# Up projection: one 512-column matmul for the high weights, the two halves of a bank added afterwards

## The chip, the cores and the metric

The kernel runs on one core of a Trainium2 chip. The metric is the device time of one execution in microseconds (us). Engines are named as in the profile: PE (matrix products), PEld (its weight loads), DVE (elementwise work on vectors), ACT (activations and casts), POOL, and SP, which issues the weight loads from memory.

## What is computed

One decoder layer on 256 tokens of width 2048. The part that matters here is the feed-forward block: the normalised rows are multiplied by `w_up` (2048 x 11264), convolved over three tokens, gated, and multiplied by `w_down`.

```python
def conv_ffn(h, w_up, ffn_conv_w, w_down):
    u = causal_dwconv3(h @ w_up, ffn_conv_w)
    g, val = jnp.split(u, 2, axis=-1)
    return (jax.nn.silu(g) * val) @ w_down
```

Before it come the modulation (`c_act @ w_mod`), the input projection, a gated convolution and linear attention, and the output projection; they are the same in both kernels.

## The kernel before

Every float32 operand is split into a high part (rounded to fp32r) and a low part (what is left), and a product is the sum of three: high weights by high activations, high weights by low activations, low weights by high activations.

The work is a list of units, run in order by `drive` (L69). A unit is one block of weights. It has `prep` (SP loads the block into one of six raw buffers, ACT casts it to the high part `wh`, one of three buffers), `low` (DVE subtracts to get the low part `wl`, one of three buffers, L145), `mm` (the products on PE) and `fin` (what follows the group's last unit, spread over the units behind it). While unit i is at its products, the list has already issued the load and cast of unit i + 2 and the low part of unit i + 1. Each engine works through its own list in order.

The up projection has 22 groups of four output tiles (4 x 128 columns of `w_up`); a group below 11 is a gate, group g + 11 its value. `up_units` (L827) makes units of four k-tiles. The activations `h2` hold two k-tiles in one buffer, each as 256 high and then 256 low columns. The products go to four PSUM banks `pss`, 256 float32 columns of each, for one group. A unit has 4 k-tiles x 4 outputs x 3 = 48 products of 256 columns (L854).

A first pass runs ten groups over k-tiles 0 to 7 (mode `part`, two units a group): their sums are copied by ACT (L795) into a buffer `part`. In the second pass these ten come back for k-tiles 8 to 15 (mode `rest`, two units): DVE adds the bank to the kept sum (L801). The other twelve groups run all 16 k-tiles in one go (mode `all`, four units) and are read straight from PSUM. The second pass goes by ORD: gate 0 and value 11 (both `rest`), gate 5 and value 16 (both `all`), 1 and 12 (`rest`), 6 and 17 (`all`), and so on. After each group come `first`, `second` and `third` of `ffn_stages` (L780), in that many following units: ACT scales the sum by the middle tap (L806), DVE adds the two other taps (`taps`, eight operations through L136, four at a time for `all`), and at the end a silu on ACT or the product of gate and value on DVE (L817).

Between these, DVE and SP also serve the modulation of later stages: a block of `w_mod` is loaded and multiplied into an accumulator (the `macc` operations through L136). One such step goes with nearly each unit of the first pass, and 16 are spread over 54 units of the second.

Of the kernel before, what the change touches and what calls it, by code (L numbers as in the profile page):

```python
# [14 lines left out]
P = 128  # L15
D = 2048
# [36 lines left out]
class Unit:  # L53
    """A weight block: load and high parts, low parts, products, and what follows them."""
# [7 lines left out]
def spread(steps, units):  # L62
    """Hands steps out evenly over the early and middle places of units."""
    places = [p for u in units for p in (u.early, u.mid)]
    for i, f in enumerate(steps):
        places[i * len(places) // len(steps)].append(f)
# [37 lines left out]
def layer_kernel(ctx: ExitStack, tc, x, c, w_mod, b_mod, mix_pre_w, mix_post_w, w_in, conv_w, gate_w2, gate_b,  # L104
# [43 lines left out]
    # ---------------------------------------------------------------- constants and small operands  # L148
# [4 lines left out]
    # ---------------------------------------------------------------- modulation: c_act @ w_mod + b_mod  # L153
# [3 lines left out]
    def mod_steps(s0, n, a, w, nj, first=False):  # L157
        """Columns a to a + w of sections s0 to s0 + n (the bias enters on partition 0), nj rows at a time."""
# [98 lines left out]
    # ---------------------------------------------------------------- the use of the modulation  # L257
    def split_acc(accs):
        """High and low parts of the accumulated sums (2048 columns)."""
# [9 lines left out]
    def mod_columns(accs, n, pre, tagname):  # L269
        """Per-partition columns of shift and scale (times the norm weight) for n k-tiles, in two steps."""  # L270
# [19 lines left out]
    def mod_rows(accs, post, tiles):  # L290
        """Gate times norm weight on all partitions: load, products and their use for each half."""
# [20 lines left out]
    # ---------------------------------------------------------------- row statistics  # L312
    def std_of(ss, n, name):
        """sqrt(sum / D + eps) from n partial sums of squares."""
# [25 lines left out]
    def turn_norm(src, kts, ps=None, ts=(0, 1)):  # L340
        """Normalised activations of up to two k-tiles, transposed, in PSUM."""
        ps = ps or bank([P, 2, T])
        for i, k in enumerate(kts):
            for t in ts:
                nc.tensor.transpose(ps[:, i, t * P:(t + 1) * P], src[t][k // 8][:, (k % 8) * P:(k % 8 + 1) * P], ident)
        return ps
# [7 lines left out]
    def act_high(kts, hf, hts):  # L354
        """High parts of up to two k-tiles; returns the two parts and their source."""
# [21 lines left out]
    # ---------------------------------------------------------------- input projection, in chunks of k  # L377
# [11 lines left out]
    def evac(ci, pair, ps):  # L389
        """Moves or adds a pair of output tiles (256 tokens each) to the accumulators."""  # L390
# [11 lines left out]
    def modulate_chunk(ci, ash, early=None):  # L402
        """Three steps: activations of a chunk and their high parts; low parts and the gate's share; its sum."""
# [83 lines left out]
    # ---------------------------------------------------------------- gated short convolution  # L487
    mts = {}

    def conv_pair(i):  # L490
        """Two channel tiles (2i, 2i + 1) of cb * conv(cc * cx), in three stages."""
# [23 lines left out]
    # ---------------------------------------------------------------- gated linear attention  # L515
# [54 lines left out]
    def gla_level(lv):  # L570
        """Stages of the scores between blocks of 2 ** lv tokens: differences, decays, products, merge.

        Decays are taken relative to the last token of the left block, so that no exponent is positive.
        One tile holds the keys of left blocks and the queries of right blocks; what else its products give is
        not taken over."""
# [74 lines left out]
    def gla_out():  # L650
        """Steps: outputs and their norms; scaling; transposes and gating in four parts."""
# [61 lines left out]
    # ---------------------------------------------------------------- output projection  # L713
# [4 lines left out]
    def z_part(t, n, ps):  # L718
        """Gated part (t, 512 columns) of the projection and its sum of squares."""
# [6 lines left out]
    def dense(ps, a, i, t, w, kk, ns, st, sp):  # L726
        """The three products of a split activation block (128 tokens) and a split weight block."""
# [47 lines left out]
    # ---------------------------------------------------------------- feed forward, up  # L775
# [4 lines left out]
    def ffn_stages(og, mode, pss):  # L780
        """Causal convolution, then silu or the product, of four output tiles (og < 11: gate)."""
# [8 lines left out]

        def first():
            if mode == "part":
                part[og] = slot([P, 4, T])
                for o in range(4):
                    nc.scalar.copy(part[og][:, o, :], pss[o])  # L795
                return
            st["u"] = pss
            if mode == "rest":
                st["u"] = [part[og][:, o, :] for o in range(4)]
                for u, ps in zip(st["u"], pss):  # L800
                    nc.vector.tensor_add(u, u, ps)  # L801
# [25 lines left out]
    def up_units(og, ks, mode):  # L827
        """4 output tiles over k-tiles ks; mode: 'part' keeps the sum, 'rest' adds it, 'all' has it whole."""
# [3 lines left out]
        def unit(k0):  # L832
# [11 lines left out]
            def mm():  # L844
                wh, wl = cur["w"]
                if k0 == ks[0]:
                    pss.extend(bank([P, T]) for _ in range(4))
                order = [(kk, o, i) for kk in range(4) for o in range(4) for i in range(3)]
                if k0 == 0:
                    order.sort(key=lambda e: (e[0] // 2, e[2]))  # L850
                for kk, o, i in order:
                    k = k0 + kk
                    w, xl = ((wh, 0), (wh, 1), (wl, 0))[i]
                    nc.tensor.matmul(pss[o], w[:, kk, o * P:(o + 1) * P], h2[k // 2][:, k % 2, xl, :],  # L854
# [349 lines left out]
```

## Time and profile before

| | |
|---|---|
| median of three runs | 1240.83 us (1240.31 to 1241.59) |
| span of the profiled execution | 1238.7 us |
| what lies around the span, against the median | 2.1 us |
| busy share of the span: PE, DVE, ACT | 96%, 74%, 45% |
| first pass of the up projection | 470.2 to 579.8 us |
| second pass | 590.3 to 990.6 us |

The profiled execution's own time is given as its span; the 2.1 us is the distance of the runs' median from it. A share of busy time is a mean over stages with different limits; the rows below take the stages apart. Matmuls are pipelined, so the distance between the starts of two of them tells their cost, and the length in a row does not.

### The profile page before, as it was taken

To read this page: it belongs to the slowest core of one execution; us is meant where nothing else is said; L and a number is where in the kernel's file an instruction comes from. 1 tells how busy PE (TensorE), PEld (TensorE's weight loads), DVE (VectorE), ACT (ScalarE), POOL (GpSimd) and SP (SyncE) were. 2 spreads that over 40 slices of the span, in tenths; PEclk is the share of its full clock that TensorE was granted. 3 is DMA by queue.
4 is the path that set the end of the run, shared out by engine and by line. 5 is a ranking of instruction groups with operands and counts; after the bars stand their busy time and mean duration, and the time that the engine had idled before them with its cause. 6 is when DMAs were issued, how large, how long until landed. Compare 5 with 4: busy or idle time off the path is not lost.

```text
span 1238.7 us, 19621 instructions
## 1 busy us (share of the span) xinstructions
PE 1192.3 (96%) x8377; PEld 1120.7 (90%) x8377; DVE 914.0 (74%) x841; ACT 558.0 (45%) x621; POOL 28.5 (2%) x49
## 2 busy tenths in 40 slices
PE   2999999999998999999999999999999999999997
PEld 1999999999996779999999999999999988888885
DVE  5899799789999889774677869596874664444454
ACT  5553333443573447443554444453443454344351
POOL 2000100100001000000000000000000000000000
PEclk9999999999999999999999999999999999999999
DMA  9999799765699997996467667676764665555521
GB/s 312 384 390 360 261 336 384 259 237 200 224 329 350 367 401 293 393 365 240 161 238 250 230 236 250 231 252 218 245 216 152 219 256 196 184 198 199 180 97 68
DMA packets 128055, 320.88 MB, mean 259 GB/s; under 512 B 8341, under 2 KB 35685, under 8 KB 118240
## 3 DMA queue, kind: packets, MB, share of 16 engines
q1 hardware_dynamic: 125360, 312.63, 70.3%
q0 software_dynamic: 2320, 6.94, 1.5%
q8 instruction: 65, 1.06, 0.3%
q14 instruction: 22, 0.18, 0.0%
q10 hardware_dynamic: 288, 0.07, 0.0%
HBM read 315.42 MB, written 4.19 MB: 258 GB/s over the span
## 4 chain that ended last, share of the span: by engine, by line
PE 87%; DVE 6%; DMA 3%; issue 2%; ACT 2%; SPq 0%; DVEq 0%; ACTq 0%
PE ps L854 41%; PE ps L730 8%; PE ps L731 8%; PE ps L729 8%; PE ps L474 6%; PE ps L476 6%; PE ps L475 6%; DMA raw<-in_w_mod_dram 3%; DVE wl L145 2%; DVE big L136 1%; PE ps L282 1%; DVE macc L136 1%; PE ps L420 1%; ACT junk L332 1%; PE ps L563 1%
## 5 line engine op out<-in xcount | busy, mean ns | idle before, releaser
L140 ACT CAST wh<-raw 128x2048 fp32r<-128x2048 f32 (+3 forms) x202 | 365.5, 1812 | 540.5 <-PE ps L854 253.0
L145 DVE TENSOR_TENSOR wl<-raw,wh 128x2048 fp32r<-128x2048 f32 (+3 forms) x202 | 437.9, 2168 | 191.7 <-ACT wh L140 191.7
L854 PE MATMUL ps<-big,wh 128*128 128x256 f32 x2816 | 473.1, 283 | 0.5 <-ACT big L360 0.5
L854 PEld LDWEIGHTS ps<-big,wh 128*128 128x128 f32 x2816 | 418.1, 192 | 1.0 <-ACT big L360 0.9
L854 PE MATMUL ps<-big,wl 128*128 128x256 f32 x1408 | 348.6, 283 | 0.0
L854 PEld LDWEIGHTS ps<-big,wl 128*128 128x128 f32 x1408 | 248.6, 192 | 0.0
L476 PE MATMUL ps<-big,wl 128*128 128x256 f32 x733 | 210.5, 287 | 2.3 <-DVE wl L145 2.3
L474 PE MATMUL ps<-big,wh 128*128 128x256 f32 x733 | 212.0, 289 | 0.2 <-ACT wh L140 0.2
L475 PE MATMUL ps<-big,wh 128*128 128x256 f32 x733 | 210.0, 287 | 0.0
L136 DVE SCALAR_TENSOR_TENSOR macc<-raw,c_act,macc 128x2048 f32<-128x2048 f32 (+1 forms) x96 | 199.4, 2077 | 4.7 <-DMA raw<-in_w_mod_dram 4.6
L730 PE MATMUL ps<-wl,big 128*128 128x512 f32 x456 | 178.7, 392 | 5.8 <-DVE wl L145 5.8
L729 PE MATMUL ps<-wh,big 128*128 128x512 f32 x456 | 178.5, 391 | 0.0
L731 PE MATMUL ps<-wh,big 128*128 128x512 f32 x456 | 178.2, 391 | 0.0
L476 PEld LDWEIGHTS ps<-big,wl 128*128 128x128 f32 x733 | 143.3, 196 | 3.2 <-DVE wl L145 3.2
L474 PEld LDWEIGHTS ps<-big,wh 128*128 128x128 f32 x733 | 143.3, 195 | 2.7 <-PE ps L420 1.3
L475 PEld LDWEIGHTS ps<-big,wh 128*128 128x128 f32 x733 | 143.4, 196 | 0.1
L730 PEld LDWEIGHTS ps<-wl,big 128*128 128x128 f32 x456 | 85.9, 188 | 25.3 <-DVE wl L145 7.6
L731 PEld LDWEIGHTS ps<-wh,big 128*128 128x128 f32 x456 | 86.0, 189 | 17.8
L729 PEld LDWEIGHTS ps<-wh,big 128*128 128x128 f32 x456 | 86.1, 189 | 17.6
L136 DVE SCALAR_TENSOR_TENSOR big<-ps,fcw,big 128x255 f32<-128x255 f32 (+1 forms) x96 | 39.5, 474 | 39.6 <-ACT big L806 39.6
L400 DVE TENSOR_TENSOR big<-big,ps 128x512 f32<-128x512 f32 x66 | 43.7, 679 | 6.6 <-PE ps L476 6.5
L136 DVE SCALAR_TENSOR_TENSOR big<-raw,c_act,big 128x1024 f32<-128x1024 f32 (+1 forms) x31 | 31.8, 1025 | 3.9 <-DMA raw<-in_w_mod_dram 3.1
(178 smaller groups left out, 645.5 us busy)
## 6 DMA issues: line engine op xcount, KB each, us to landing
raw<-in_w_up_dram SPq DMA_DIRECT2D x88, 1024.0 KB, 5.0
raw<-in_w_mod_dram SPq DMA_DIRECT2D x64, 1024.0 KB, 7.1
raw<-in_w_down_dram SPq DMA_DIRECT2D x44, 1024.0 KB, 4.8
raw<-in_w_in_dram SPq DMA_DIRECT2D x24, 960.0 KB, 6.7
raw<-in_w_mod_dram SPq DMA_DIRECT2D x32, 640.0 KB, 7.6
raw<-in_w_out_dram SPq DMA_DIRECT2D x16, 1024.0 KB, 7.6
raw<-in_w_in_dram SPq DMA_DIRECT2D x12, 1024.0 KB, 7.7
raw<-in_w_mod_dram SPq DMA_DIRECT2D x22, 512.0 KB, 6.8
```

What stands on the lines that cost most here:

```text
L136: nc.vector.scalar_tensor_tensor(o, a, s, b, op0=op0, op1=op1)
L140: nc.scalar.copy(hi, raw)
L145: nc.vector.tensor_sub(lo, raw, hi.bitcast(F32))
L282: nc.tensor.matmul(o, t[:, cs], r[:, 0:2], start=j == 0, stop=j == len(terms) - 1)
L400: nc.vector.tensor_add(dst, dst, ps)
L474: nc.tensor.matmul(ps, w[0][:, kk, cs], ht[:, k % 2, 0, :], start=st, stop=False)
L475: nc.tensor.matmul(ps, w[0][:, kk, cs], ht[:, k % 2, 1, :], start=False, stop=False)
L476: nc.tensor.matmul(ps, w[1][:, kk, cs], ht[:, k % 2, 0, :], start=False, stop=sp)
L729: nc.tensor.matmul(ps, a[:, i, 0, ts_], w[0][:, kk, ns], start=st, stop=False)
L730: nc.tensor.matmul(ps, a[:, i, 0, ts_], w[1][:, kk, ns], start=False, stop=False)
L731: nc.tensor.matmul(ps, a[:, i, 1, ts_], w[0][:, kk, ns], start=False, stop=sp)
L854: nc.tensor.matmul(pss[o], w[:, kk, o * P:(o + 1) * P], h2[k // 2][:, k % 2, xl, :], start=(k == ks[0] and i == 0), stop=(k == ks[-1] and ...
```

## The change

High weights now multiply the 256 high and the 256 low columns of a k-tile in one product of 512 columns, which fills a whole PSUM bank: half 0 holds the sums over high activations, half 1 those over low ones. The low weights' product (256 columns) goes to half 1. The two halves have to be added when the group ends: in `part` and `all` ACT copies half 1 of the four banks to a buffer and DVE adds half 0 (`summed`); in `rest` DVE adds half 1 and then half 0 to the kept sum. In `all` what follows reads that buffer, not PSUM. Only the first two k-tiles of the very first unit keep the separate products of 256 columns.

```diff
+        def summed(dst):
+            for o in range(4):
+                nc.scalar.copy(dst[:, o, :], pss[o][:, 1, :])
+            for o in range(4):
+                nc.vector.tensor_add(dst[:, o, :], dst[:, o, :], pss[o][:, 0, :])
+
         def first():
             if mode == "part":
                 part[og] = slot([P, 4, T])
-                for o in range(4):
-                    nc.scalar.copy(part[og][:, o, :], pss[o])
+                summed(part[og])
                 return
-            st["u"] = pss
             if mode == "rest":
-                st["u"] = [part[og][:, o, :] for o in range(4)]
-                for u, ps in zip(st["u"], pss):
-                    nc.vector.tensor_add(u, u, ps)
+                u = part[og]
+                for half in (1, 0):
+                    for o in range(4):
+                        nc.vector.tensor_add(u[:, o, :], u[:, o, :], pss[o][:, half, :])
+            else:
+                u = slot([P, 4, T])
+                summed(u)
+            st["u"] = [u[:, o, :] for o in range(4)]
...
-                    pss.extend(bank([P, T]) for _ in range(4))
-                order = [(kk, o, i) for kk in range(4) for o in range(4) for i in range(3)]
-                if k0 == 0:
-                    order.sort(key=lambda e: (e[0] // 2, e[2]))
-                for kk, o, i in order:
+                    pss.extend(bank([P, 2, T]) for _ in range(4))
...
+                for kk in range(2 * apart, 4):
                     k = k0 + kk
-                    w, xl = ((wh, 0), (wh, 1), (wl, 0))[i]
-                    nc.tensor.matmul(pss[o], w[:, kk, o * P:(o + 1) * P], h2[k // 2][:, k % 2, xl, :],
-                                     start=(k == ks[0] and i == 0), stop=(k == ks[-1] and i == 2))
+                    for o in range(4):
+                        cs = slice(o * P, (o + 1) * P)
+                        nc.tensor.matmul(pss[o], wh[:, kk, cs], h2[k // 2][:, k % 2, :, :],
+                                         start=(first and kk == 0), stop=False)
+                        nc.tensor.matmul(pss[o][:, 1, :], wl[:, kk, cs], h2[k // 2][:, k % 2, 0, :],
+                                         start=False, stop=(last and kk == 3))
```

On PE, in the second unit of the first group (`big` is a pair of k-tiles of the activations, `ps` the bank of one output tile), one k-tile of four outputs stood before as:

```order
L854 MATMUL ps_4406<-big_4395,wh_4368 128x256 x2
L854 MATMUL ps_4406<-big_4395,wl_4388 128x256
L854 MATMUL ps_4407<-big_4395,wh_4368 128x256 x2
L854 MATMUL ps_4407<-big_4395,wl_4388 128x256
L854 MATMUL ps_4408<-big_4395,wh_4368 128x256 x2
L854 MATMUL ps_4408<-big_4395,wl_4388 128x256
```

and now stands as:

```order
L871 MATMUL ps_4406<-big_4395,wh_4368 128x512
L873 MATMUL ps_4406<-big_4395,wl_4388 128x256
L871 MATMUL ps_4407<-big_4395,wh_4368 128x512
L873 MATMUL ps_4407<-big_4395,wl_4388 128x256
L871 MATMUL ps_4408<-big_4395,wh_4368 128x512
L873 MATMUL ps_4408<-big_4395,wl_4388 128x256
```

Two products with the same weights have become one of twice the columns: 4224 products of 256 columns in the whole up projection become 1400 of 512 and 1424 of 256. Where a unit starts at k-tile 0, the products with `wl` stood behind sixteen with `wh`; now the second product of every unit but the first asks for `wl`.

On DVE, in the second pass behind a pair of `all` groups, at the end of a value group in mode `rest` (`big_5456`, now `big_5220`, is its kept sum), there stood before:

```order
L801 TENSOR_TENSOR big_5456<-big_5456,ps_8060 128x256
L801 TENSOR_TENSOR big_5456<-big_5456,ps_8061 128x256
L801 TENSOR_TENSOR big_5456<-big_5456,ps_8062 128x256
L801 TENSOR_TENSOR big_5456<-big_5456,ps_8063 128x256
L136 SCALAR_TENSOR_TENSOR macc_5964<-raw_8252,c_act,macc_5964 128x2048
L145 TENSOR_TENSOR wl_8259<-raw_8184,wh_8186 128x2048
```

and now:

```order
L807 TENSOR_TENSOR big_5220<-big_5220,ps_7258 128x256
L807 TENSOR_TENSOR big_5220<-big_5220,ps_7259 128x256
L807 TENSOR_TENSOR big_5220<-big_5220,ps_7260 128x256
L807 TENSOR_TENSOR big_5220<-big_5220,ps_7261 128x256
L807 TENSOR_TENSOR big_5220<-big_5220,ps_7258 128x256
L807 TENSOR_TENSOR big_5220<-big_5220,ps_7259 128x256
L807 TENSOR_TENSOR big_5220<-big_5220,ps_7260 128x256
L807 TENSOR_TENSOR big_5220<-big_5220,ps_7261 128x256
L136 SCALAR_TENSOR_TENSOR macc_5632<-raw_7410,c_act,macc_5632 128x2048
L145 TENSOR_TENSOR wl_7417<-raw_7354,wh_7356 128x2048
```

Four additions more stand ahead of the modulation step and of the next low part. In `part` and `all` four additions are new on DVE, ahead of the next low part, and in `all` four copies on ACT.

## Rows read from the trace of the kernel before

**Rows 1.** Page: engine totals, and the costliest DVE addition from PSUM (512 columns).
```profile
PE 1192.3 (96%) x8377; PEld 1120.7 (90%) x8377; DVE 914.0 (74%) x841; ACT 558.0 (45%) x621; POOL 28.5 (2%) x49
...
L400 DVE TENSOR_TENSOR big<-big,ps 128x512 f32<-128x512 f32 x66 | 43.7, 679 | 6.6 <-PE ps L476 6.5
```

**Rows 2.** Windows: both passes, one stretch of the second, a slow-clock stretch.
```profile
core 0: us, PE busy (x) PEld busy (x) DVE busy (x) ACT busy (x) POOL busy (x), PEclk, DMA share, GB/s
470.20:579.80 109.60, 109.60 (x912) 109.50 (x912) 81.78 (x40) 53.31 (x67) 0.00 (x0) 1.00 0.93 346
590.30:990.60 400.30, 400.30 (x3321) 399.94 (x3320) 290.80 (x313) 181.87 (x180) 0.53 (x1) 1.00 0.63 222
804.60:839.10 34.50, 34.50 (x289) 34.50 (x289) 32.17 (x42) 17.18 (x19) 0.00 (x0) 1.00 0.68 243
...
585.00:590.00 5.00, 5.00 (x25) 5.00 (x26) 0.24 (x2) 3.05 (x4) 0.00 (x0) 0.50 0.93 359
```

**Rows 3.** Chain that ended last, second pass: start, us, what.
```profile
590.63 369.60 PE ps L854 x3072
```

**Rows 4.** Timeline of PE: end of the up, start of the down projection (start, length).
```profile
985.21 0.28 PE L854 MATMUL ps<-big,wl 128*128 128x256 f32 x1
...
990.61 0.28 PE L854 MATMUL ps<-big,wl 128*128 128x256 f32 x1
...
991.20 0.39 PE L731 MATMUL ps<-wh,big 128*128 128x512 f32 x1
...
1003.45 0.39 PE L731 MATMUL ps<-wh,big 128*128 128x512 f32 x1
```

**Rows 5.** Timeline of DVE behind two groups in mode `all`.
```profile
806.93 1.65 DVE L136 SCALAR_TENSOR_TENSOR big<-ps,fcw,big 128x255 f32<-128x255 f32 x4 [3.84 <-ACT big L806]
808.50 2.28 DVE L145 TENSOR_TENSOR wl<-raw,wh 128x2048 fp32r<-128x2048 f32 x1
810.70 2.35 DVE L136 SCALAR_TENSOR_TENSOR macc<-raw,c_act,macc 128x2048 f32<-128x2048 f32 x1
812.97 1.65 DVE L136 SCALAR_TENSOR_TENSOR big<-ps,fcw,big 128x255 f32<-128x255 f32 x4
...
816.73 1.22 DVE L817 TENSOR_TENSOR big<-big,big 128x1024 f32<-128x1024 f32 x1
817.86 1.40 DVE L801 TENSOR_TENSOR big<-big,ps 128x256 f32<-128x256 f32 x4
819.19 2.28 DVE L145 TENSOR_TENSOR wl<-raw,wh 128x2048 fp32r<-128x2048 f32 x1
821.39 3.24 DVE L136 SCALAR_TENSOR_TENSOR big<-big,fcw,big 128x255 f32<-128x255 f32 x8
824.55 2.28 DVE L145 TENSOR_TENSOR wl<-raw,wh 128x2048 fp32r<-128x2048 f32 x1
...
835.75 2.28 DVE L145 TENSOR_TENSOR wl<-raw,wh 128x2048 fp32r<-128x2048 f32 x1
```

**Rows 6.** Timeline of ACT: a group's copies, and the stretch of rows 5.
```profile
575.87 1.19 ACT L795 COPY big<-ps 128x256 f32<-128x256 f32 x4
...
804.63 1.90 ACT L140 CAST wh<-raw 128x2048 fp32r<-128x2048 f32 x1 [3.86 <-PE ps L854]
806.43 1.56 ACT L806 ACTIVATE big<-ps,fcw 128x256 f32<-128x256 f32 x4
810.39 1.91 ACT L140 CAST wh<-raw 128x2048 fp32r<-128x2048 f32 x1 [2.39 <-PE ps L854]
```

**Rows 7.** Timelines at the first pass's third unit: its low part, its first products.
```profile
478.03 2.28 DVE L145 TENSOR_TENSOR wl<-raw,wh 128x2048 fp32r<-128x2048 f32 x1
...
481.82 2.08 PE L854 MATMUL ps<-big,wh 128*128 128x256 f32 x16
```

**Rows 8.** Windows: a stretch of the first pass, columns as in rows 2.
```profile
500.00:510.00 10.00, 10.00 (x85) 10.00 (x85) 8.11 (x5) 3.39 (x7) 0.00 (x0) 1.00 1.04 393
```

More of the change, by code (lines that the diff above doesn't have):

```diff
@@ L846, in mm @@
                 if k0 == ks[0]:
-                    pss.extend(bank([P, T]) for _ in range(4))
-                order = [(kk, o, i) for kk in range(4) for o in range(4) for i in range(3)]
-                if k0 == 0:
-                    order.sort(key=lambda e: (e[0] // 2, e[2]))
-                for kk, o, i in order:
-                    k = k0 + kk
-                    w, xl = ((wh, 0), (wh, 1), (wl, 0))[i]
-                    nc.tensor.matmul(pss[o], w[:, kk, o * P:(o + 1) * P], h2[k // 2][:, k % 2, xl, :],
-                                     start=(k == ks[0] and i == 0), stop=(k == ks[-1] and i == 2))
+                    pss.extend(bank([P, 2, T]) for _ in range(4))
+                first, last = k0 == ks[0], k0 + 4 > ks[-1]
+                apart = k0 == 0 and og == 0
+                if apart:
+                    for i in range(3):
+                        for kk in range(2):
+                            for o in range(4):
+                                w, xl, half = ((wh, 0, 0), (wh, 1, 1), (wl, 0, 1))[i]
+                                nc.tensor.matmul(pss[o][:, half, :], w[:, kk, o * P:(o + 1) * P],
+                                                 h2[0][:, kk, xl, :], start=(kk == 0 and i == 0), stop=False)
+                for kk in range(2 * apart, 4):
+                    k = k0 + kk
+                    for o in range(4):
+                        cs = slice(o * P, (o + 1) * P)
[3 more added lines that the diff above has]
+                                         start=False, stop=(last and kk == 3))
             return Unit(prep, lows, mm, ffn_stages(og, mode, pss) if k0 + 4 > ks[-1] else [])
```

## The prediction, made before the changed kernel was run

> **What bounds the kernel now.** I read the engine totals first: PE is busy 96% of the span, DVE 74% [rows 1]. That is a mean over stages, so next the windows of the two passes that the change touches: PE is busy for all of 109.6 us and all of 400.3 us at the full granted clock, and DVE for 81.8 and 290.8 us of them [rows 2]. A busy PE may still be one that waits inside a matmul, so third the chain of waits: over the second pass it is one piece, 3072 products of L854 in 369.60 us, with no other engine in it [rows 3]. The up projection is a row of matmuls that waits for nothing, 3072 in 369.60 us or 120.3 ns each, and what a matmul costs there is paid in full.
>
> **What the change removes.** The price of a matmul is the distance of starts. From 985.21 to 990.61 us lie 45 products of 256 columns: 5.40 / 45 = 120.0 ns. From 991.20 to 1003.45 us, in the down projection, lie 54 of 512 columns: 12.25 / 54 = 226.85 ns [rows 4]. At the granted 2.4 GHz the columns alone take 106.7 and 213.3 ns, so both sizes carry about 13.4 ns more, whatever their length. A merge replaces two of 256 by one of 512 and drops one such part: 240.0 - 226.85 = 13.15 ns. There are 1400 merges (1408 pairs less the eight kept apart in the first unit): 18.4 us. With the 120.3 ns of the chain it would be 13.75 ns and 19.3 us, the upper bound; the lower is no gain at all, if the new form of product (two pieces of 256 columns side by side, which no row shows) ran as two. I take 13.15, since the merged operand lies as one run of 512 columns, like the one in the down projection.
>
> The Trainium skill, "TensorE: Matmul & The Clock Gate", section "Back-to-back issue gap", speaks against most of this: it gives the isolated warm gap as columns / 2.4 plus 2.5 ns, so a merge would save 2.5 ns, 1400 of them 3.5 us. By that rule the estimate is 1237.3 us instead of what the rows give. The trace disagrees at both sizes: 13.4 ns stand where the page has 2.5.
>
> A unit so shrinks from 48 x 120.0 = 5.76 us (the casts that wait for PE stand 804.63 and 810.39 [rows 6]) to 16 x (226.85 + 120.0) = 5.55 us.
>
> **What it adds.** On DVE, additions of 256 columns: four at the end of each of ten `part` and twelve `all` groups, and eight instead of four in ten `rest` groups, 128 more than before. Four advance DVE by 819.19 - 817.86 = 1.33 us [rows 5]. The second pass gets 22 times four, 29.3 us, and DVE would be busy 290.8 + 29.3 = 320 us of 386 (400.3 less 68 units times 0.21), 83%; the first gets ten times four, 13.3 us, and comes to 95 us of 105, 90%. On ACT, 48 copies, four for 1.19 us [rows 6], 14 us; ACT has half its time free [rows 2]. Two waits are new: DVE's additions wait for ACT's copies, with modulation steps and low parts queued behind them on DVE, and for these PE waits; and in `all` ACT's scaling waits for the additions, with the next cast of weights behind it. Also, where a unit starts at k-tile 0, `wh` was last used by the 40th of 48 products and now is by the last but one, so the cast that waits for the buffer starts 5.43 instead of 4.80 us into the unit; the low parts of [rows 5] had over 5 us to spare (that of c ends at 810.8 us, for a start at 816.0). In the mean DVE takes the additions. But its load isn't even, and PE waits as soon as one low part is late.
>
> So I follow the tightest stretch, where DVE is busy 32.2 of 34.5 us [rows 2]: a value group in `all` ends, then a gate and a value in `rest`, with two modulation steps between. Time 0 is 804.5 us, the start of unit a. Steps from one start to the next [rows 5]: low part 2.20, modulation step 2.27, half the taps 1.57, all of them 3.16, gate times value 1.13, four additions 1.33. New at the head: ACT's cast and then the copies (806.43 - 804.63 = 1.80 behind the cast, then 1.19), the additions behind the first copy, done at 3.75, and the scaling behind them; the first taps end at 5.5, where they ended at 4.0. Then: low part of c 7.7 (unit c starts at 11.1), modulation 10.0, taps 11.5, low d 13.7 (16.6), product 14.9, eight additions 17.5, low e 19.7 (22.2), taps 22.9, low f 25.1 (27.7), eight additions 27.8, modulation 30.0, low g 32.2 (33.3), taps 35.4, low h 37.6 (38.8). The least that is left is 1.1 us, at g. Before, the low part of h stood at 838.0 us [rows 5], 33.5 on this clock, for a start at 40.3: 6.8 us to spare. So the cover is nearly used up and holds. The same walk gives 1.2 us in one more such stretch and about 3 us in the two with one modulation step fewer. In the two groups of `all` behind each, eight units with 20 us less of it, DVE catches up. Banks are no problem: in this walk the additions end 3.75 us after an `all` group and at most 6.4 us after a `rest` group, and the bank's next group starts 11.1 us after that end.
>
> In the first pass the third unit is the tight place. Its low part ends at 480.31 us and its products start at 481.82 [rows 7], 0.3 us earlier after the change, and now ask for the low part with the second product: 1.2 us are left. The memory traffic there rises too: a block of `w_up` and one of `w_mod` a unit, 2.097 MB, are 378 GB/s at 5.55 us; 393 GB/s are shown at a full DMA share [rows 8], which makes 5.34 us a unit. It stays behind PE, by 0.2 us. Both I cost at nothing; if either cover were gone, 0.2 us a unit over 20 units would be 4 us.
>
> The stretch between the passes, where the clock fell to half [rows 2], moves 4 us ahead. If the slow clock meets more or less of the work, a 5 us stretch at half clock is worth 2.5 us, either way.
>
> **Sum.** 1238.7 - 18.4 = 1220.3 us of span, with the 2.1 us by which the runs' median lies above it 1222.4 us.
>
> **Rivals.**
> 1. DVE's low parts come late in the tight stretches. Until g there are 20 additions; each that costs x more than 0.33 takes 20x from 1.1 us. A lone one lasts 1.40 - 3 x 0.33 = 0.41 us; if none overlapped, 1.6 - 1.1 = 0.5 us would be lost in two stretches, 1 us in all. At 0.50 us an addition it is 2.3 us in two and 0.3 in two, 5.2 us: 1227.6 us. For it speaks that the second four additions write over what the first four have just written; against it that taps do the same at a distance of two and advance at 0.40 us each.
> 2. The merged product costs two old ones, because the 13.4 ns go with each 256-column piece of an activation tile and not with the matmul: 1240.8 us, no change. Against it stands that 256 and 512 columns pay the same part in these rows, with different operands on the moving side.
> 3. The other sign: DVE takes PE's place. With 20 additions in each of four stretches the loss is 80x less the spares 1.1, 1.2, 3 and 3; it eats the 18.4 us at x = 0.335, an addition of 0.67 us. The addition of twice the columns takes 0.68 us [rows 1], so it would need that every half cost as much as a whole. At 0.75 us: 80 x 0.42 - 8.3 = 25 us, 1247.5 us.
> 4. More gain: the short product behind a long one starts with its weights long in place and loses its 13.4 ns too: another 18.8 us, 1203.7 us. Against it the down projection, where every load has a long product to hide behind and the part is there all the same [rows 4].
>
> **Chances.** The sum 0.80 (its own range 1220 to 1225: the bounds 18.4 and 19.3 us, the clock's 2.5 us to the bad side, half of it to the good). Rival 1 0.11, rival 2 0.04, rival 3 0.02, rival 4 0.03. The range of eight in ten takes in most of rival 1 and the clock: 1219 to 1229 us. The measurement tells a change of over 0.2%, about 2.5 us, from none. Faster: 0.80 + 0.11 + 0.03 = 0.94; same 0.04; slower 0.02.
>
> **What would show it.** In the changed profile: starts of a 512- and a 256-column product together 347 ns apart, at full clock; units of 5.55 us between the casts that wait for PE; PE's waits for DVE's low parts none or below 2 us in all; DVE advancing about 2.7 us over eight additions; the low part ahead of unit g just over 1 us early; and the second pass's 68 units at that pace. Wrong would make it a pair at 360 ns or more (the price itself), a PE that waits for `wl` at the end of each `rest` pair, or casts that wait for memory in the first pass.

## The result, and the profile after

The changed kernel takes 1225.88 us (median of 1223.84, 1224.61, 1227.15 and 1233.59) against 1240.57 us before on the same chip: a ratio of 0.9896 with a 95% interval of 0.9864 to 0.9928. Later 12 more of its runs were timed in two sets. Of all 16, eight lie at 1223.84 to 1227.15 us (mean 1225.0, the lower group), eight at 1230.19 to 1233.59 us (mean 1232.2, the upper group), and none between. The prediction was 1222.4 us; neither group is there, and what makes two of them became the main question. Of these 16 runs three were profiled.

The page's totals, its rows on the two products, and its row on the additions behind the copies:

```profile
span 1222.1 us, 17086 instructions
...
PE 1172.9 (96%) x6977; PEld 1042.0 (85%) x6977; DVE 954.8 (78%) x969; ACT 573.4 (47%) x669; POOL 28.5 (2%) x49
...
L871 PE MATMUL ps<-big,wh 128*128 128x512 f32 x1400 | 488.4, 393 | 0.0
L873 PE MATMUL ps<-big,wl 128*128 128x256 f32 x1400 | 392.6, 280 | 0.0
...
L796 DVE TENSOR_TENSOR big<-big,ps 128x256 f32<-128x256 f32 x88 | 31.2, 417 | 46.1 <-ACT big L794 46.1
```

Against [rows 1]: 1400 products fewer on PE, 128 instructions more on DVE and 48 on ACT, and PE stood idle ahead of neither product of the up projection (0.0). The windows, first pass and the middle of the second, show the same engine full and DVE closer to it than in [rows 2]:

```profile
core 0: us, PE busy (x) PEld busy (x) DVE busy (x) ACT busy (x) POOL busy (x), PEclk, DMA share, GB/s
470.20:575.00 104.80, 104.53 (x599) 91.01 (x600) 92.51 (x73) 52.36 (x66) 0.00 (x0) 1.00 0.99 359
600.00:940.00 340.00, 340.00 (x1964) 299.78 (x1963) 284.38 (x366) 172.02 (x193) 0.00 (x0) 1.00 0.70 239
```

The second row gives the price of a pair in one line: 1964 products are 982 pairs in 340 us, 346 ns each (the rims add part of a product). The timeline of PE shows it sharper, and shows that the first pass is different. From 500.01 and from 699.71 us to the last row of each piece lie 20 pairs:

```profile
500.01 0.40 PE L871 MATMUL ps<-big,wh 128*128 128x512 f32 x1
500.25 0.28 PE L873 MATMUL ps<-big,wl 128*128 128x256 f32 x1
500.37 0.40 PE L871 MATMUL ps<-big,wh 128*128 128x512 f32 x1
500.61 0.28 PE L873 MATMUL ps<-big,wl 128*128 128x256 f32 x1
500.73 0.40 PE L871 MATMUL ps<-big,wh 128*128 128x512 f32 x1
500.96 0.28 PE L873 MATMUL ps<-big,wl 128*128 128x256 f32 x1
501.07 0.40 PE L871 MATMUL ps<-big,wh 128*128 128x512 f32 x1
...
507.09 0.40 PE L871 MATMUL ps<-big,wh 128*128 128x512 f32 x1
...
699.71 0.39 PE L871 MATMUL ps<-big,wh 128*128 128x512 f32 x1
699.94 0.28 PE L873 MATMUL ps<-big,wl 128*128 128x256 f32 x1
...
706.64 0.39 PE L871 MATMUL ps<-big,wh 128*128 128x512 f32 x1
```

In the first pass 7.08 / 20 = 0.354 us, in the second 6.93 / 20 = 0.3465 us. Over whole bursts (rows of pairs that nothing interrupts) a pair takes 0.3533 and 0.3467 us. At a granted clock of 1.00, 2.4 GHz, that is 848 and 832 cycles on average. I call them the long and the short rhythm. The short one is even: the 256-column product starts 0.2300 us behind the 512-column one, and the next pair 0.1167 us behind that. The long one is a cycle of three unequal pairs, 350, 361 and 349 ns from start to start, repeated without a break; the three pairs from 500.01 to 501.07 us are one such cycle, 1.06 us where the short rhythm takes 1.04. On average the 256-column product follows there after 0.236 to 0.237 us and is itself followed after 0.117.

The tightest stretch, which the prediction walked through, in the timeline of DVE, with the first products of unit g from that of PE:

```profile
808.91 2.74 DVE L807 TENSOR_TENSOR big<-big,ps 128x256 f32<-128x256 f32 x8
811.56 2.30 DVE L145 TENSOR_TENSOR wl<-raw,wh 128x2048 fp32r<-128x2048 f32 x1
...
824.02 2.32 DVE L145 TENSOR_TENSOR wl<-raw,wh 128x2048 fp32r<-128x2048 f32 x1
```

```profile
827.63 0.39 PE L871 MATMUL ps<-big,wh 128*128 128x512 f32 x1
827.86 0.28 PE L873 MATMUL ps<-big,wl 128*128 128x256 f32 x1
```

Eight additions advance DVE by 811.56 - 808.91 = 2.65 us. The low part of g is done at 826.34 us, 1.3 us ahead of the unit and 1.5 us ahead of the product that reads it. In the list of waits from 470 to 975 us PE never waits for a `wl` of L145. So the cover held, nearly as narrow as walked.

One wait of PE did grow. The products of L282, which stand ahead of the last unit of the first pass, read a `wh` that ACT casts into one of the same three buffers (L264). The timeline of PE, before and after:

```profile
580.08 0.27 PE L282 MATMUL ps<-ones_r,wh 128*128 128x2 f32 x1 [0.18 <-ACT wh L264]
```

```profile
579.33 0.27 PE L282 MATMUL ps<-ones_r,wh 128*128 128x2 f32 x1 [1.06 <-ACT wh L264]
```

That is 0.9 us more, once. The cast of L264 starts where the unit's last product with `wh` ends, at 578.98 us before (its sixteen last products with `wh` ran to 578.94 us) and at 578.23 us after (its last one ran from 577.75 to 578.15 us). That product was the unit's 40th of 48 and now is its last but one.

### The profile page after: what moved, and what is told of

Same layout as the page of the kernel before. It is cut to its first block, busy times and chain, and to the rows that moved or that the text cites. A ratio compares the mean times of both kernels' runs of the same rounds, so it can differ in the third digit from the quotient of the medians.

```text
span 1222.1 us, 17086 instructions
## 1 busy us (share of the span) xinstructions
PE 1172.9 (96%) x6977; PEld 1042.0 (85%) x6977; DVE 954.8 (78%) x969; ACT 573.4 (47%) x669; POOL 28.5 (2%) x49
## 4 chain that ended last, share of the span: by engine, by line
PE 90%; DVE 3%; DMA 3%; ACT 2%; issue 2%; SPq 0%; DVEq 0%; ACTq 0%
PE ps L871 26%; PE ps L873 14%; PE ps L730 9%; PE ps L731 9%; PE ps L729 8%; PE ps L474 6%; PE ps L476 6%; PE ps L475 6%; DMA raw<-in_w_mod_dram 3%; PE ps L563 1%; PE ps L471 1%; DVE big L136 1%; PE ps L282 1%; DVE wl L145 1%; PE ps L420 1%
## 5 line engine op out<-in xcount | busy, mean ns | idle before, releaser
L145 DVE TENSOR_TENSOR wl<-raw,wh 128x2048 fp32r<-128x2048 f32 (+3 forms) x202 | 438.3, 2171 | 136.6 <-ACT wh L140 136.5
L871 PE MATMUL ps<-big,wh 128*128 128x512 f32 x1400 | 488.4, 393 | 0.0
L873 PE MATMUL ps<-big,wl 128*128 128x256 f32 x1400 | 392.6, 280 | 0.0
L871 PEld LDWEIGHTS ps<-big,wh 128*128 128x128 f32 x1400 | 262.6, 188 | 59.3
L873 PEld LDWEIGHTS ps<-big,wl 128*128 128x128 f32 x1400 | 265.0, 189 | 0.0
L476 PE MATMUL ps<-big,wl 128*128 128x256 f32 x733 | 209.9, 286 | 3.6 <-DVE wl L145 3.6
L474 PE MATMUL ps<-big,wh 128*128 128x256 f32 x733 | 211.3, 288 | 0.2 <-ACT wh L140 0.2
L475 PE MATMUL ps<-big,wh 128*128 128x256 f32 x733 | 209.3, 286 | 0.0
L476 PEld LDWEIGHTS ps<-big,wl 128*128 128x128 f32 x733 | 142.6, 195 | 4.8 <-DVE wl L145 4.8
L474 PEld LDWEIGHTS ps<-big,wh 128*128 128x128 f32 x733 | 142.6, 194 | 2.7 <-PE ps L420 1.3
L475 PEld LDWEIGHTS ps<-big,wh 128*128 128x128 f32 x733 | 142.7, 195 | 0.1
L136 DVE SCALAR_TENSOR_TENSOR big<-big,fcw,big 128x254 f32<-128x254 f32 (+1 forms) x176 | 72.3, 485 | 0.0
L796 DVE TENSOR_TENSOR big<-big,ps 128x256 f32<-128x256 f32 x88 | 31.2, 417 | 46.1 <-ACT big L794 46.1
```

Source lines behind the costliest of these rows:

```text
L136: nc.vector.scalar_tensor_tensor(o, a, s, b, op0=op0, op1=op1)
L145: nc.vector.tensor_sub(lo, raw, hi.bitcast(F32))
L474: nc.tensor.matmul(ps, w[0][:, kk, cs], ht[:, k % 2, 0, :], start=st, stop=False)
L475: nc.tensor.matmul(ps, w[0][:, kk, cs], ht[:, k % 2, 1, :], start=False, stop=False)
L476: nc.tensor.matmul(ps, w[1][:, kk, cs], ht[:, k % 2, 0, :], start=False, stop=sp)
L871: nc.tensor.matmul(pss[o], wh[:, kk, cs], h2[k // 2][:, k % 2, :, :], start=(first and kk == 0), stop=False)
```

## Experiments

All times are medians; each set was run on one chip beside the kernel before, whose median there is given.

**The change again** (nothing edited). 

> The changed kernel once more, with nothing altered, to narrow its interval and to see a second execution's trace. Its first trace showed pairs (a 512- and a 256-column product) 0.3533 us apart all through the first pass and 0.3467 us all through the second. If the first pass's pairs are longer because of what that pass does (its memory traffic or its groups in two parts), the same two numbers come again in the same places, and the ratio stays at 0.989 to 0.991. If each burst of products falls by chance into one of two rhythms, either pass can show either number; a second pass at 0.3533 would add 1088 x 6.7 ns = 7.3 us, and would explain runs of the changed kernel near 1233 us.

Measured 1227.8 us (1223.87 to 1233.26, six runs) against 1238.66 us, ratio 0.9912 (0.9884 to 0.9939). The profiled run took 1230.19 us, and its second pass is in the long rhythm up to the products of L305 and L306, to be seen in the window and in 20 pairs of the timeline of PE:

```profile
600.00:940.00 340.00, 340.00 (x1927) 294.83 (x1926) 281.42 (x362) 169.77 (x192) 0.00 (x0) 1.00 0.69 237
```

```profile
699.97 0.40 PE L871 MATMUL ps<-big,wh 128*128 128x512 f32 x1
...
707.04 0.40 PE L871 MATMUL ps<-big,wh 128*128 128x512 f32 x1
```

Same program, same clock, no wait, 37 products fewer in 340 us: 7.07 / 20 = 0.3535 us a pair. Behind the products of L305 and L306 the last 80 pairs of this trace are in the short rhythm (20 of them from 952.36 to 959.30 us, 0.347 us each). The long burst between the products of L282 and those of L305 (the last unit of the first pass and 63 of the second) holds 1024 pairs; 1024 x 6.67 ns = 6.8 us is about the distance at which the two groups of runs lie (7.2 us between their means). That every run of the upper group was in the long rhythm there is inferred: of that group this one alone was profiled.

**Without the loads of the second modulation set.** 

> The second set of modulation steps, which fall into the first pass of the up projection, no longer loads its blocks of w_mod: each step reads its own accumulator in their place (so the modulation of the feed forward is left out). VectorE's work stays and the memory traffic of the first pass falls by about half. If the traffic makes the first pass's pairs long, they go to 0.3467 us, and the pass is about 20 x 16 x 6.7 ns = 2.1 us shorter: about 1222 to 1224 us. If it is the mode of the groups or a chance of rhythm, pairs of 0.3533 us stay and the time with them. If a cast waited for memory there, more than 2.1 us comes back.

```diff
-    f2, fsteps2 = mod_steps(3, 2, 1024, 1024, 1)
+    f2, fsteps2 = mod_steps(3, 2, 1024, 1024, 1, dry=True)
...
```

(With `dry` a step issues no load and reads `cur["acc"]` in the block's place.) Measured 1227.51 us (1223.32 to 1229.89) against 1238.66 us, ratio 0.9904 (0.9882 to 0.9925): as the change. The window of the first pass, and 20 pairs each of the first pass, the second, and the end of the second:

```profile
470.20:575.00 104.80, 104.30 (x598) 90.49 (x597) 92.88 (x72) 52.37 (x65) 0.00 (x0) 1.00 0.61 196
```

```profile
499.95 0.40 PE L871 MATMUL ps<-big,wh 128*128 128x512 f32 x1
...
507.02 0.40 PE L871 MATMUL ps<-big,wh 128*128 128x512 f32 x1
...
699.66 0.40 PE L871 MATMUL ps<-big,wh 128*128 128x512 f32 x1
...
706.59 0.40 PE L871 MATMUL ps<-big,wh 128*128 128x512 f32 x1
...
949.79 0.40 PE L871 MATMUL ps<-big,wh 128*128 128x512 f32 x1
...
956.85 0.40 PE L871 MATMUL ps<-big,wh 128*128 128x512 f32 x1
```

The traffic is down from 359 to 196 GB/s and the rhythm of the first pass is still the long one (0.3535): the traffic is not its cause. In neither trace does the list of waits show a cast that waited for memory there. In this trace the rhythm also changes within the second pass, from 0.3465 to 0.353 us, the other way round from the trace before, and again across the eight products of L305 and L306 (944.75 to 946.4 us), the only other work on PE in that pass.

**TensorE's part alone.** 

> TensorE's part of the change alone: the merged products stay, but the half of a bank that holds the low activations' sum is never added (these parts of the up projection are left out), and ScalarE's and VectorE's lists are those of the kernel before. If the 128 additions and 48 copies are covered, as the prediction has it, this is no faster than the changed kernel: ratio to the kernel before 0.985 to 0.991, pairs at 0.3467 us in the second pass. If part of the gain is lost to late low parts (rival 1), it is faster than the changed kernel by that part: up to 5 us at 0.50 us an addition, 1219 to 1221 us. If the additions cost nothing but the first pass's pairs are long because VectorE reads PSUM and SBUF more, the first pass's pairs go to 0.3467 us here.

```diff
-                nc.scalar.copy(dst[:, o, :], pss[o][:, 1, :])
-            for o in range(4):
-                nc.vector.tensor_add(dst[:, o, :], dst[:, o, :], pss[o][:, 0, :])
+                nc.scalar.copy(dst[:, o, :], pss[o][:, 0, :])
...
-                for half in (1, 0):
+                for half in (0,):
...
-                u = slot([P, 4, T])
-                summed(u)
-            st["u"] = [u[:, o, :] for o in range(4)]
+                u = None
+            st["u"] = [u[:, o, :] if u is not None else pss[o][:, 0, :] for o in range(4)]
```

Measured 1224.42 us (1223.3 to 1225.5, four runs) against 1238.66 us, ratio 0.9882 (0.9869 to 0.9896). The window answers to those above:

```profile
600.00:940.00 340.00, 340.00 (x1963) 299.82 (x1962) 258.71 (x286) 158.43 (x152) 0.00 (x0) 1.00 0.71 241
```

DVE has 26 us less to do in it, and PE passes 1963 products where the change in its short rhythm passed 1964. In this window the additions and copies are covered, wholly. The median lies lower than the change's, and all four runs lie close to the change's lower group; that the additions choose the rhythm can't be excluded by four runs. The first pass is in the long rhythm here too, with no addition in it, so the additions don't make it.

**The added work alone.** 

> The added work alone: the bank's two halves, the 128 additions and the 48 copies stay as in the changed kernel, but each product of 512 columns is made as two of 256, one for each half, as in the kernel before. If the whole gain comes from the price of a product, 1400 products of 226.7 ns are 2800 of 120.0 again, units take 5.76 us, and the time is that of the kernel before within 0.2% (ratio 0.998 to 1.002). If writing to two halves in turn or the additions cost TensorE something, it is slower than the kernel before by that.

```diff
-                        nc.tensor.matmul(pss[o], wh[:, kk, cs], h2[k // 2][:, k % 2, :, :],
-                                         start=(first and kk == 0), stop=False)
+                        for xl in range(2):
+                            nc.tensor.matmul(pss[o][:, xl, :], wh[:, kk, cs], h2[k // 2][:, k % 2, xl, :],
+                                             start=(first and kk == 0 and xl == 0), stop=False)
```

Measured 1240.99 us (1239.34 to 1243.3, ten runs) against 1239.3 us, ratio 1.0017 (1.0006 to 1.0029). The timeline of PE, 111 groups of three products between the two rows:

```profile
700.00 0.40 PE L872 MATMUL ps<-big,wh 128*128 128x256 f32 x2
...
739.96 0.40 PE L872 MATMUL ps<-big,wh 128*128 128x256 f32 x2
```

39.96 / 111 = 0.3600 us, three times the 120.0 ns of [rows 4]. Every gain is gone with the merge: it came from the price of a product. The 1.7 us on top are at the edge of what the measurement tells. The traces place most of it: PE waits 1.06 us for the `wh` of L264 ahead of the products of L282, as in the change, where it waited 0.18 us before, and from the last product ahead of those to the first behind the transposes it takes 12.01 us instead of 10.66. The two spans differ by 1.4 us.

**Additions twice.** 

> Each added addition is made twice (eight instead of four behind a group that is copied first, sixteen instead of eight behind the last part of a group), so the sums of the low parts count double. By the walk of the prediction the tightest stretches hold 20 additions ahead of their last low part, now 40: 20 x 0.33 = 6.6 us later against 1.1 to 1.3 us of spare in two stretches and about 3 us in two others, so PE should now wait for wl at the ends of these stretches, 5.4 us in each of two and 3.6 us in each of two, 18 us in all: about 1244 us, as slow as the kernel before or slower. If the walk is too tight (the stretches catch up more than it allows), the loss is below 8 us. If the additions are nowhere near the path, nothing changes: 1224 to 1227 us.

```diff
+            for o in range(4):
+                nc.vector.tensor_add(dst[:, o, :], dst[:, o, :], pss[o][:, 0, :])
...
-                for half in (1, 0):
+                for half in (1, 0, 1, 0):
```

Measured 1244.58 us (1242.85 to 1245.33) against 1238.66 us, ratio 1.0043 (1.0029 to 1.0057), 16.8 us above the change's median of 1227.8 us in this set. The list of waits from 470 us on, then the timeline of PE at unit g of the tight stretch, and the low part that it waited for, in that of DVE:

```profile
PE ps L875 <- DVE wl L145: 12.7, 9, 3.8
```

```profile
843.51 0.58 PE L875 MATMUL ps<-big,wl 128*128 128x256 f32 x1 [3.75 <-DVE wl L145]
```

```profile
841.18 2.27 DVE L145 TENSOR_TENSOR wl<-raw,wh 128x2048 fp32r<-128x2048 f32 x1
```

Rival 3 of the prediction, made real: the low part ends at 843.45 us and the product that needs it starts behind it. 16.8 us were lost where 18 were expected. The nine waits hold 12.7 us of idle time, and across them the starts of the products lie 15.3 us further apart than nine pairs of 0.35 us. Behind each wait the pairs go on in a rhythm of their own: of the nine stretches of 32 pairs and more between interruptions, from the products of L282 on, four are in the long one and five in the short (two of 16 pairs are in the long one too). So the kernel was a few additions from its limit, and the limit stood where the walk had put it.

**Order by k-tile: four products of 512, then four of 256.** 

> The same products as in the changed kernel, but within a k-tile the four of 512 columns come first and the four of 256 after them, where they alternated. The traces so far show two rhythms of an alternating pair, 0.3467 and 0.3533 us, set anew at each interruption and kept until the next. If the second rhythm belongs to the alternation, the eight products now always take 4 x 0.3467 = 1.387 us, in both passes of every run: 1221.5 to 1224 us, runs within 3 us of each other, first pass 2.1 us shorter than so far. If each group of products finds its phase by itself, 1.387 and 1.413 us both appear, within one burst too. If a change between sizes costs a product, the groups are shorter than 1.387 us, with 2 changes in 8 products and not 8: down to 4 x (0.2267 + 0.1133) = 1.36 us and 1214 us.

```diff
                 for kk in range(2 * apart, 4):
-                    for o in range(4):
-                        long(kk, o); short(kk, o)
+                    for f in (long, short):
+                        for o in range(4):
+                            f(kk, o)
```

(`long` and `short` stand for the two products of the diff ahead.) Measured 1229.35 us (1227.35 to 1229.4, four runs) against 1239.3 us, ratio 0.9919 (0.9904 to 0.9934). The timeline of PE over one k-tile:

```profile
700.89 1.09 PE L869 MATMUL ps<-big,wh 128*128 128x512 f32 x4
701.82 0.64 PE L874 MATMUL ps<-big,wl 128*128 128x256 f32 x4
702.29 1.09 PE L869 MATMUL ps<-big,wh 128*128 128x512 f32 x4
```

A k-tile takes 702.29 - 700.89 = 1.40 us in both passes, where I expected 1.387 (1.400 to 1.406, on average 1.403). The second rhythm is gone, and the runs lie within 2.1 us; but going from 512 to 256 and back costs some 17 ns here, once a k-tile. All three of my expectations were wrong on that.

**Order by unit: sixteen of 512, then sixteen of 256.** 

> All sixteen products of 512 columns of a unit first, then its sixteen of 256, so that a low part of the weights is asked for 16 x 0.2267 = 3.6 us later in the unit. If the second rhythm belongs to the alternation, units take 16 x (0.2267 + 0.1200) = 5.55 us everywhere and the time is 1221.5 to 1224 us in all runs, a median some 2 to 4 us below that of the changed kernel. If lateness of low parts cost nothing before, as the trace shows, the room of 3.6 us buys nothing by itself. If rhythm is kept in this order too, both 5.55 and 5.65 us appear and the median stays at 1226 to 1228 us.

```diff
-                for kk in range(2 * apart, 4):
-                    for o in range(4):
-                        long(kk, o); short(kk, o)
+                for f in (long, short):
+                    for kk in range(2 * apart, 4):
+                        for o in range(4):
+                            f(kk, o)
```

Measured 1221.64 us (1221.06 to 1225.03) against 1239.3 us, ratio 0.9866 (0.9848 to 0.9885). The timeline of PE over one unit:

```profile
700.33 3.82 PE L869 MATMUL ps<-big,wh 128*128 128x512 f32 x16
703.98 2.08 PE L874 MATMUL ps<-big,wl 128*128 128x256 f32 x16
705.89 3.82 PE L869 MATMUL ps<-big,wh 128*128 128x512 f32 x16
```

5.56 us a unit, in both passes (5.567 on average): 16 x (0.2267 + 0.1200) = 5.547 and some 20 ns for the one change of size and back. In the trace these lie at the head of the blocks: the first five products of 512 columns are followed after 233, 236, 228, 232 and 231 ns, all others after 226.7, and the first two of 256 after 113 and 119 ns instead of 120.

**Additions twice, in the order by unit.** 

> Each addition made twice (the sums of the low parts count double) in the order with all 512-column products of a unit first. The doubled additions cost 18 us when the low part was asked for with the unit's second product, through PE's waits for wl. By the walk, the low part may now come 16 x 0.2267 = 3.6 us later: 6.6 - 1.2 - 3.6 = 1.8 us are left in two stretches and nothing in the two with about 3 us of spare, so some 4 us are lost: 1226 to 1229 us. If the loss of the doubled additions lay anywhere else than in the late low part (a bank not free, activations not ready), the time stays near 1244 us.

The two edits shown above together. Measured 1221.45 us (1220.33 to 1222.78) against 1239.3 us, ratio 0.9858 (0.9841 to 0.9876): not 4 us lost but none, and PE never waits for a `wl` of L145. The low part of unit g in the timeline of DVE, and the unit's two blocks of products in that of PE:

```profile
826.38 2.28 DVE L145 TENSOR_TENSOR wl<-raw,wh 128x2048 fp32r<-128x2048 f32 x1
```

```profile
825.25 3.82 PE L871 MATMUL ps<-big,wh 128*128 128x512 f32 x16
828.91 1.34 PE L876 MATMUL ps<-big,wl 128*128 128x256 f32 x10
```

(Ten of its sixteen short products fall into that view.) The low part comes in time by 828.91 - 828.66 = 0.25 us. What my sum had left out is in the timeline of ACT. First the change, then this kernel, at the head of the same stretch:

```profile
794.43 1.91 ACT L140 CAST wh<-raw 128x2048 fp32r<-128x2048 f32 x1 [3.64 <-PE ps L871]
796.24 1.18 ACT L794 COPY big<-ps 128x256 f32<-128x256 f32 x4
```

```profile
790.14 1.91 ACT L140 CAST wh<-raw 128x2048 fp32r<-128x2048 f32 x1 [3.65 <-PE ps L871]
791.95 1.19 ACT L794 COPY big<-ps 128x256 f32<-128x256 f32 x4
```

By the unit, `wh` is free after the sixteenth product. The cast is all but done when the group ends (791.86 us, six units of 5.565 us ahead of 825.25), and the copies start 0.1 us behind that end; in the change they start 1.9 us behind it (794.35 us, six units of 5.547 us ahead of 827.63). So room grows by 1.8 us at the head besides the 3.4 us at the end (3.66 us ahead of the first `wl` product instead of 0.23). 1.5 us of room in the change - 20 x 0.33 + 3.4 + 1.8 = 0.1 us, beside the 0.25 us measured.

**Both orders side by side.** 

> The changed kernel a third time, on the same chip and beside the order by units, for a direct comparison. With the rhythm of each burst set anew, runs should fall into groups: 1022 alternating pairs of the long burst of the second pass at 0.3467 or 0.3533 us make 6.8 us between two runs, so times near 1224 and near 1231 us both come, a spread of at least 6 us over ten runs. If the spread had another cause than the rhythm, the profiled run's time doesn't go with the rhythm that its trace shows.

> The order by units once more beside the changed kernel. In its first trace a unit took 5.565 us everywhere (16 x 0.2267 + 16 x 0.1200 is 5.547; two changes of size cost some 0.018 us a unit). If that order has no second rhythm, the up projection takes 503 us as in the first trace, the times are 1220 to 1225 us, and the median lies 3 to 6 us below that of the changed kernel on this chip. If units of 5.65 us turn up, or the spread is as wide as the changed kernel's, it has the second rhythm too and its first result was luck.

On one chip, with the kernel before at 1239.97 us: the change 1231.08 us (1224.47, 1225.88, 1230.79, 1231.36, 1232.11, 1233.34), ratio 0.9914 (0.989 to 0.9938); the order by unit 1221.46 us (1219.7 to 1222.89, five runs), ratio 0.9845 (0.9827 to 0.9862). The change's six runs fall into the same two groups. Its profiled run is the one of 1225.88 us; its window, and that of the order by unit:

```profile
600.00:940.00 340.00, 340.00 (x1964) 299.78 (x1963) 286.48 (x368) 170.71 (x192) 0.00 (x0) 1.00 0.69 239
```

```profile
600.00:940.00 340.00, 340.00 (x1955) 300.46 (x1954) 284.00 (x366) 170.71 (x192) 0.00 (x0) 1.00 0.68 238
```

1964 products: the short rhythm, in a run of the lower group, as in the first trace; the one profiled run of the upper group had 1927. The order by unit passes 1955, a little less than the best rhythm, and no trace of it shows the worse one. It beats the change by 9.6 us of the medians on this chip, more than the 3 to 6 expected, since four of the change's six runs were of the upper group; but even the change's fastest run is slower than its slowest. Its distance to the change's two runs in the lower group, 3.7 us, does not come from the price of the products. Between the passes, from the last product ahead of L282 to the first behind the transposes, the two traces take 6.45 us by unit and 11.39 in the change: PE waits there 0.5 us instead of 2.1, since `wh` is free earlier, and the clock stood at half for 3.4 us instead of 10.2. In the two other traces of the order by unit that stretch takes 9.3 us and the half clock lasts 6.8.

## Why the prediction was right, and where it was not

**The price of a product** was the step that carried everything, and its mechanism is shown: each product of this kernel carries about 13 ns beyond its columns, one of two goes with a merge, and with the merge undone and all else kept the gain is gone. In the short rhythm a pair takes 0.3467 us where the sum had 0.3469 (226.85 + 120.0 ns), and a unit 838.80 - 833.25 = 5.55 us between two casts of ACT that wait for PE, as predicted (timeline of ACT):

```profile
833.25 1.92 ACT L140 CAST wh<-raw 128x2048 fp32r<-128x2048 f32 x1 [3.58 <-PE ps L871]
838.80 1.92 ACT L140 CAST wh<-raw 128x2048 fp32r<-128x2048 f32 x1 [3.63 <-PE ps L871]
```

The rule of the Trainium skill for an isolated product ("TensorE: Matmul & The Clock Gate", "Back-to-back issue gap"), which was weighed against it, would by estimate have given 3.5 us; the measured ratio of 0.9896 is 12.9 us of 1240.57.

**What failed** is one thing in that step: "The price of a matmul is the distance of starts", with both prices taken from runs of products of one size and added. A row that alternates between sizes has a price of its own, and two of them. In the long rhythm a pair costs 0.3533 us on average and a merge saves 6.7 ns and not 13.15. The first pass was in it in all six traces of alternating pairs: its 296 pairs up to the products of L282 saved 2.0 us and not 3.9, which no rival had. The second pass is in it in some executions, and then the long burst of 1024 pairs gives back 6.8 us. The forecast thus holds for half the runs only, and is for them 2.6 us too low (1225.0 against 1222.4); the other half lies at 1230 us and more, beyond the range. The median of the four runs lies within it because three of them were of the lower group, and that was luck.

In the first trace itself the span fell by 16.6 us. The 1104 pairs behind the products of L282 make 1104 x 13.3 ns = 14.7 us of it and the 296 ahead of them 2.0 us, 16.7 together. What else moved nearly cancels. The slow clock between the passes lasted 6.8 us instead of 10.2 (granted clock 0.50), an estimated 1.7 us to the good at half speed and within the 2.5 us allowed for either side; PE's longer wait ahead of L282 takes back 0.9. Another trace of the change had 10.2 us of slow clock there too, so this gain is not the change's own. A stretch of slow clock ahead of the first pass lasted 6.8 us in some traces of alternating pairs and 13.7 in others, but the last product ahead of L282 starts at 578.0, 578.3 and 578.6 us in the former and at 577.5, 578.5 and 579.6 in the latter: it does not tell the runs apart. What spreads the runs within each group stays open.

**The added work** was costed at nothing. For the additions and copies that is shown: 1963 products against 1964 in the same window with the additions left out and in. DVE came to 83.6% of that window for the 83% worked out; eight additions took 2.65 us for 2.7; the low part of g was 1.3 us early for 1.1; PE waited for no `wl` of L145. Rival 1 is out, each addition advances DVE by 0.33 us. Not free was the later release of `wh`, which the prediction saw and costed at nothing too: at one place, the products of L282, PE waits 0.9 us longer behind it. With the additions left out it waits there as well (1.02 us), and with the order by unit, where `wh` is free after the sixteenth product, that wait is gone.

**Rival 3** is no fact of this change but its distance is measured: 20 additions more in the tight stretches, and the time is above that of the kernel before (1244.58 against 1238.66 us). **Rival 2** is out by the window and by the undone merge. **Rival 4** is out in its size: a short product behind a long one does start its successor 3.3 ns sooner than 120.0, but the long one takes 3.3 ns more than 226.7 in the short rhythm and some 10 on average in the long one, so nothing is left of it. Memory stayed behind PE in the first pass, and half the traffic changed nothing.

**Open** is what decides the rhythm. Shown is that it is kept through a burst, up to 1024 pairs, and that where it changed there had been an interruption of the pairs: the products of L282 and the transposes between the passes, those of L305 and L306, PE's waits in the kernel with doubled additions. Memory traffic does not make the first pass long, and neither do the additions. The granted clock is 1.00 in both rhythms, and the clock at a burst's start doesn't choose: the burst behind the transposes began at half clock and went long in one trace and short in three, and began at full clock and went long in one and short in one. The traces of orders in groups of four or sixteen show one pace only. Why the first pass was always long, and what holds up every third pair, no run tells.

## What to carry to other kernels

Where PE is full and each product carries a fixed part, merging products that share their weights pays by the number dropped; take the part from the distances of starts at two sizes, not from busy times. Don't add prices from uniform runs to get that of a mixture: put products of one size together (here by unit, which gave 1221.5 us beside the change's 1231.1, or beside 1225 in its lower group), which also lets the late operand come later and frees the early operand's buffer sooner. And when the runs of one kernel fall into two groups, count the products in the same window of a trace of each before taking a median of them.

## What the hardware showed that I had not expected

- An alternating row of 512- and 256-column products ran at 832 or, on average, 848 cycles a pair (0.3467 or 0.3533 us at a granted clock of 1.00), the same program in the same place, fixed from one interruption to the next. The slower pace is a cycle of three pairs (350, 361 and 349 ns), the faster one is even.
- A change of product size has a price: about 17 ns for a change to 256 and back in groups of four (1.403 us a k-tile beside 1.387) and about 20 in groups of sixteen (5.567 us a unit beside 5.547), where it sits in the first five products of 512 columns; and none in the short rhythm of single pairs.
- The clock stayed at half between the passes for 10.2 us before, and for 6.8 or 10.2 us in different executions of the change. In the kernel with doubled additions PE waited 3.75 us, and in the last half microsecond of that wait, from 843.0 us, the granted clock fell to 0.50 for 3.4 us: the 512-column product at 843.89 us took 0.63 us instead of 0.39.
